# Weight sums of a seven-product up projection: from VectorE to accumulating DMAs, and one product accumulated onto another's negative

## The chip, the cores and the metric

The kernel runs on one core of one Trainium2 chip. The metric is the time of one execution in device microseconds (us). The engines in the profile: PE is TensorE (matmuls; PEld its weight loads), DVE is VectorE, ACT is ScalarE, POOL is GpSimd, SP is SyncE, which issues nearly all DMAs.

## The reference

One inference step of a decoder with two layers, for a prompt of 1024 positions and 8 samples of 8 positions, 1088 columns in all; the model has 1024 rows. Each layer is a mixer (layer 0: convolution and retention, layer 1: a gated recurrence), then a gated feed-forward network (FFN) with a causal depthwise convolution of width 3 between its projections. The change touches only the first product of the FFN, `h @ w_up`, and the RMS norm in front of it:

```python
def _conv_ffn(h, buf, w_up, conv_w, conv_b, w_down):
    z = h @ w_up
    zc, new_buf = _causal_dwconv(z, buf, conv_w, conv_b)
    g, u = jnp.split(zc, 2, axis=-1)
    return (jax.nn.gelu(g) * u) @ w_down, new_buf
...
        x = x + y
        hn = _rmsnorm(x, p['norm_ffn'][l])
        y, fb = _conv_ffn(hn, ffn_buf[l], p['w_ffn_up'][l], p['ffn_conv_w'][l], p['ffn_conv_b'][l], p['w_ffn_down'][l])
```

`w_up` is 1024 x 5632: 22 blocks of 128 columns for g and 22 for u.

## The kernel before, in words

**Exact products.** All data is fp32. A value is split into a high part (a ScalarE copy to fp32r) and a low part (VectorE: the value less its high part), and a product is three matmuls: high x high, high x low, low x high (`mm3`, L227; each matmul is issued at L222). So each weight tile of 128 x 512 costs one ScalarE copy (L119) and one VectorE subtraction (L137, or L167 in the up stage).

**The up stage with seven products.** A pair p takes the blocks p (g) and 22 + p (u) of `w_up`, each 128 x 1024 for the two halves of the 1024 rows: a11, a12 (rows' halves of the first block) and a21, a22 (of the second). The activations are halved in the same way by rows and by columns (544 columns each). This is a 2 x 2 block product, done by Winograd's form of Strassen's scheme with 7 products in place of 8, each on sums of weight blocks and sums of activation blocks. One product is four row blocks of 128, so 12 matmuls of 272 columns, done for each of two ranges of columns (sb 0 and 1): 168 matmuls a pair, and there are 22 pairs in a layer.

**Weight sums.** `Pair.steps` (L161) loads both blocks into `raw` tiles (L124, by SP; three such buffers) and makes seven weight tiles W[0] to W[6] in turn, one a `yield`: a11; a11 - a21; a21 + a22; a21 + a22 - a11; a12; a22; a12 less the fourth. The sums are VectorE adds on 128 x 512 (L172, L175, L180, L185). While pair p is multiplied, pair p + 1's weights are made: three during the first `four`, four during the second (`make_first`, `make`).

**Activation sums.** `norm_halves` (L316) normalises one of three column blocks (208, 208, 128 columns of each half): ScalarE squares and VectorE sums (L331), TensorE transposes the sums (L341), VectorE reduces (L342), ScalarE takes the root (L343), VectorE the reciprocal (L344), TensorE broadcasts it (L351), VectorE scales X (L357), and then four splits and three sums or more per row group follow (`put`, `diff`; L368, L369, L374). The plain blocks go to HB, the sums to HX.

**Products.** `four` (L524) does the products of W[0] to W[3] of one column range, `three` (L546) those of W[4] to W[6], which accumulate onto banks of the first four (p1, p7, p5). MOVE (L484) says which activation block goes with which weight. After the first product ScalarE copies its bank into u2 (L530) and W[4]'s product may then accumulate onto the bank; after the fourth, VectorE adds: u2 += p6 (L540), u3 = u2 + p7 (L541), and the results z are written by L511, L513, L553, L556.

**What sets the order.** The code is written in program order with `side` generators that are advanced by a count of matmuls; a scheduler then orders each engine's instructions by priority and by what is free. Each engine runs its own in order, and so does the queue of DMAs that each issues. The FFN starts while the last block of the projection before it is still being normalised: `proj_tail` (L405) calls `ffn.start()` (both `raw` loads of pair 0), makes the first weights during its third block, and appends the norms of blocks 0, 1 and 2 to `side`. At L588 the rest of pair 0's weights are made, all norms but the last are finished, and the first products run beside block 2's norm. Since `three` of pair 0 stands ahead of the second `four` there (L620 to L624), block 2's norm ends between them.

**Banks.** PSUM has five banks in pool mmp and three in axp, the latter also used by the transposes of the norms.

## Time and profile before

| | us |
|---|---|
| median of 3 runs (lowest, highest) | 2309.07 (2307.93, 2309.26) |
| the profiled execution | 2310.94 |
| its span | 2309.2 |
| up stage, steady part, layer 0 and layer 1 | 527 to 970 and 1592 to 2035 |
| start of the up stage, layer 0 and layer 1 | about 485 to 527 and 1552 to 1592 |

The span is what the trace covers, 1.7 us less than the time measured for the same execution; its mean TensorE clock was 0.989 of full speed. Rows of the trace give a start in us from the span's start, a duration in us, the engine, the line of the kernel, the operation, out<-in by the program's names, the size, and in brackets how long the engine had waited and for what. Durations of neighbouring VectorE and ScalarE instructions overlap by some hundredths or tenths of a us, so the step from one start to the next is the cost of one in a row.

### The profile page before, as it was taken

What the parts mean: (1) busy time and instruction counts of PE and PEld (TensorE: products, weight loads), DVE (VectorE), ACT (ScalarE), POOL (GpSimd) and SP (SyncE); (2) the same over time, 40 slices, a digit from 0 to 9 for tenths busy, and PEclk for the clock granted to TensorE, in tenths of its full rate; (3) what the DMA queues carried; (4) which work ended last, traced back from release to release, by engine and by line L of the source; (5) the groups of instructions that cost most, each with busy time, mean ns of one, the idle gap of its engine ahead of it and who ended that gap; (6) DMA issues with size and microseconds to landing.
All of it is one profiled execution on the core that took longest, in us unless ns stands there. A gap on an engine that the chain in (4) does not pass through costs nothing.

```text
span 2309.2 us, 38057 instructions
## 1 busy us (share of the span) xinstructions
PE 2265.7 (98%) x15428; PEld 2230.5 (97%) x15428; DVE 1650.1 (71%) x2945; ACT 1018.6 (44%) x2082; POOL 37.5 (2%) x65
## 2 busy tenths in 40 slices
PE   9999999989999999999999999999999999999998
PEld 8999999979999999999999999998999999999998
DVE  6899975499888888844337766569888888763425
ACT  6344436445444444622125766435454444442212
POOL 0000000000000000000000121000000000000000
PEclk9999999989999999999999999999999999999999
DMA  5212113222221222454123111422322221264302
GB/s 196 68 40 69 45 55 97 74 67 85 95 85 67 75 85 80 152 169 138 58 74 105 37 38 46 124 73 62 110 68 75 85 84 67 84 210 138 97 19 78
DMA packets 114672, 200.37 MB, mean 87 GB/s; under 512 B 27136, under 2 KB 81280, under 8 KB 114368
## 3 DMA queue, kind: packets, MB, share of 16 engines
q1 hardware_dynamic: 114496, 197.94, 27.2%
q8 instruction: 121, 1.98, 0.4%
q14 instruction: 55, 0.45, 0.1%
HBM read 151.70 MB, written 46.21 MB: 86 GB/s over the span
## 4 chain that ended last, share of the span: by engine, by line
PE 90%; DVE 6%; ACT 2%; DMA 1%; issue 1%; DVEq 0%; SPq 0%; ACTq 0%
PE mm L222 72%; PE ax L222 14%; DVE X L357 1%; DVE acc L331 1%; DVE HB L369 0%; DVE td L374 0%; PE ax L1190 0%; DVE xe L1075 0%; PE ax L882 0%; DVE HX L369 0%; PE ax L873 0%; DMA X<-in_x 0%; PE ax L864 0%; PE ax L844 0%; PE ax L832 0%
## 5 line engine op out<-in xcount | busy, mean ns | idle before, releaser
L222 PE MATMUL mm<-HB,ws 128*128 128x384 f32 (+4 forms) x9504 | 1536.7, 317 | 12.9 <-ACT HB L368 5.6
L222 PEld LDWEIGHTS mm<-HB,ws 128*128 128x128 f32 x9504 | 1464.3, 189 | 27.1 <-ACT HB L368 7.8
L119 ACT ACTIVATE ws<-raw 128x512 fp32r<-128x512 f32 x472 | 289.1, 620 | 337.4 <-PE mm L222 232.0
L167 DVE TENSOR_TENSOR ws<-raw,ws 128x512 fp32r<-128x512 f32 x264 | 180.1, 686 | 71.6 <-ACT ws L119 69.4
L222 PE MATMUL mm<-HX,ws 128*128 128x272 f32 x1584 | 228.0, 293 | 0.3 <-ACT HX L368 0.2
L222 PE MATMUL ax<-HX,ws 128*128 128x272 f32 x1584 | 222.6, 289 | 0.0
L222 PEld LDWEIGHTS mm<-HX,ws 128*128 128x128 f32 x1584 | 212.6, 193 | 1.5 <-ACT HX L368 0.8
L222 PEld LDWEIGHTS ax<-HX,ws 128*128 128x128 f32 x1584 | 208.1, 188 | 0.0
L137 DVE TENSOR_TENSOR ws<-raw,ws 128x512 fp32r<-128x512 f32 x208 | 135.5, 665 | 79.2 <-ACT ws L119 78.5
L263 DVE TENSOR_TENSOR X<-X,mm 128x384 f32<-128x384 f32 (+1 forms) x132 | 69.7, 529 | 150.9 <-PE mm L222 142.5
L750 DVE SCALAR_TENSOR_TENSOR X<-U,par,X 128x1024 f32<-128x1024 f32 x120 | 151.3, 1275 | 0.0
L222 PE MATMUL ax<-HB,ws 128*128 128x272 f32 x1056 | 145.5, 287 | 0.0
L222 PE MATMUL mm<-A,ws 128*128 128x384 f32 (+1 forms) x864 | 142.7, 327 | 0.0
L222 PEld LDWEIGHTS mm<-A,ws 128*128 128x128 f32 x864 | 142.4, 188 | 0.0
L222 PEld LDWEIGHTS ax<-HB,ws 128*128 128x128 f32 x1056 | 136.9, 188 | 0.0
L566 DVE SCALAR_TENSOR_TENSOR X<-X,par 128x1104 f32<-128x1104 f32 x88 | 119.7, 1360 | 0.7 <-ACT X L565 0.5
L565 ACT ACTIVATE X<-X,par 128x1104 f32<-128x1104 f32 x88 | 114.3, 1298 | 5.6 <-DVE X L556 5.6
L567 DVE SCALAR_TENSOR_TENSOR X<-X,par 128x1104 f32<-128x1104 f32 x88 | 116.6, 1360 | 0.0
L553 ACT ACTIVATE X<-mm 128x272 f32<-128x272 f32 x88 | 35.0, 397 | 180.2 <-PE mm L222 180.2
L572 ACT ACTIVATE X<-X 128x1024 f32<-128x1024 f32 x44 | 46.7, 1061 | 45.0 <-DVE X L567 45.0
L500 ACT ACTIVATE X<-fst 128x16 f32<-128x16 f32 x88 | 18.3, 213 | 96.8 <-DVE X L567 96.8
L586 DVE TENSOR_TENSOR A<-yl,A 128x544 fp32r<-128x544 f32 x24 | 17.4, 725 | 60.3 <-ACT A L585 60.3
(236 smaller groups left out, 1929.3 us busy)
## 6 DMA issues: line engine op xcount, KB each, us to landing
raw<-in_w SPq DMA_DIRECT2D x176, 512.0 KB, 3.8
yd<-X SPq DMA_DIRECT2D x44, 544.0 KB, 2.7
yl<-yd SPq DMA_DIRECT2D x88, 272.0 KB, 3.4
spf<-X SPq DMA_DIRECT2D x4, 1664.0 KB, 6.9
xr<-spf SPq DMA_DIRECT2D x32, 208.0 KB, 3.0
raw<-in_w SPq DMA_DIRECT2D x16, 384.0 KB, 4.1
X<-in_xt SPq DMA_DIRECT2D x8, 512.0 KB, 7.1
X<-in_x SPq DMA_DIRECT2D x4, 768.0 KB, 5.3
```

What stands on the lines that cost most here:

```text
L119: nc.scalar.activation(hi, src, AF.Copy)
L137: nc.vector.tensor_tensor(lo, src, hi.bitcast(F32), ALU.subtract)
L167: nc.vector.tensor_tensor(lo, src, hi.bitcast(F32), ALU.subtract)
L222: nc.tensor.matmul(out, lhsT, rhs, start=start, stop=stop, skip_group_check=more)
L263: nc.vector.tensor_tensor(X[:, m, t0:t0 + n], X[:, m, t0:t0 + n], ps[:, :n], ALU.add)
L331: nc.vector.tensor_tensor(acc[:, :N], acc[:, :N], sq[:, :N], ALU.add)
L553: nc.scalar.activation(low(z1, sb), p1[:, :n], AF.Copy)
L565: nc.scalar.activation(y, z[:, 2:NE], AF.Identity, bias=pc(fb, f), scale=pc(fw, 2 * 44 + f))
L566: v.scalar_tensor_tensor(y, z[:, 1:NE - 1], pc(fw, 44 + f), y, ALU.mult, ALU.add)
L567: v.scalar_tensor_tensor(y, z[:, 0:NE - 2], pc(fw, f), y, ALU.mult, ALU.add)
L572: nc.scalar.activation(YG[:, :NP], y[:, :NP], AF.Gelu_apprx_tanh)
L750: nc.vector.scalar_tensor_tensor(cv, U[i][:, j:j + NP], wj, cv, ALU.mult, ALU.add)
```

## The change

Three things, in `Pair`, `norm_halves` and `four`/`three`.

1. The weight sums are made by DMAs that GpSimd issues with `accum_op=ALU.add`: each reads 128 x 512 of a weight block from DRAM and adds it onto half a `raw` tile. There are four a pair, here called A to D. To have sums only, the scheme's signs change: W[0] to W[6] are a11; a21 + a22 (A is issued when the pair is loaded); a11 + a21 (B, after W[0] is split); a11 + a21 + a22 (C, after W[1] is split); a12; a22; the sum of all four (D, after W[3] is split). The four VectorE adds and the tile s3 are gone. Primes (w0', w1') mark the weights of the pair after the one that is multiplied.
2. The activation sums change sign with them (`diff` takes an operation), and W[1] and W[2] change places in MOVE.
3. For pairs from the third on, ScalarE copies the negated bank of W[0]'s product, a, into the bank b (L547 after the change), W[3]'s product accumulates onto it, and ScalarE copies b out as u (L549). For the first two pairs, W[3]'s product has its own bank; ScalarE copies it into u3 (L544) and VectorE forms u = u3 - a (L545). The VectorE add L540 and the copy L530 are gone. W[4]'s product still accumulates onto a.

```diff
+            self.add(1, 0, 1, 1)
             self.gen = self.steps()
 
+        def part(self, j, h):
+            return self.raws[j][:, h * 512:(h + 1) * 512]
+
+        def add(self, j, h, q, g):
+
+            nc.gpsimd.dma_start(self.part(j, h), I["w"][self.i + q][:, g * 512:(g + 1) * 512], accum_op=ALU.add)
+
+        def put(self, j, h):
+            src = self.part(j, h)
+            w, hi, lo = split_w(src)
+            nc.vector.tensor_tensor(lo, src, hi.bitcast(F32), ALU.subtract)
+            self.w.append(w)
+
         def steps(self):
...
-            v.tensor_tensor(s3, a11, a21, ALU.subtract)
-            put(a11)
+            self.put(0, 0)
+            self.add(0, 0, 1, 0)
             yield
-            v.tensor_tensor(a21, a21, a22, ALU.add)
-            put(s3)
+            self.put(1, 0)
+            self.add(1, 0, 0, 0)
             yield
-            put(a21)
+            self.put(0, 0)
             yield
-            v.tensor_tensor(a11, a21, a11, ALU.subtract)
-            put(a11)
+            self.put(1, 0)
+            self.add(1, 0, 0, 1)
             yield
-            put(a12)
+            self.put(0, 1)
             yield
-            v.tensor_tensor(a12, a12, a11, ALU.subtract)
-            put(a22)
+            self.put(1, 1)
             yield
-            put(a12)
+            self.put(1, 0)
...
-            MOVE = (0, 5, 1, 4, 2, 6, 3)
+            MOVE = (0, 1, 5, 4, 2, 6, 3)
...
-                p1 = bank()
-                product(W.w[0], 0, sb, p1, True)
-                nc.scalar.activation(u2[:, :n], p1[:, :n], AF.Copy)
+                a = bank()
+                product(W.w[0], 0, sb, a, True)
                 after(0)
...
-                p6 = bank2() if sb else bank()
-                product(W.w[3], 3, sb, p6, True)
-                v.tensor_tensor(u2[:, :n], u2[:, :n], p6[:, :n], ALU.add)
-                v.tensor_tensor(u3[:, :n], u2[:, :n], p7[:, :n], ALU.add)
-                high(z2, sb, u3, p5)
+                b, u = bank2(), u2s[sb]
+                if p < 2:
+
+                    product(W.w[3], 3, sb, b, True)
+                    nc.scalar.activation(u3[:, :n], b[:, :n], AF.Copy)
+                    v.tensor_tensor(u[:, :n], u3[:, :n], a[:, :n], ALU.subtract)
+                else:
+                    nc.scalar.activation(b[:, :n], a[:, :n], AF.Copy, scale=-1.0)
+                    product(W.w[3], 3, sb, b)
+                    nc.scalar.activation(u[:, :n], b[:, :n], AF.Copy)
+                v.tensor_tensor(u3[:, :n], u[:, :n], f[:, :n], ALU.add)
+                high(z2, sb, u3, e, ALU.subtract)
```

Line numbers shift: L222 becomes L225, L167 (low half) becomes L172, and L167 is now the accumulating DMA; L331 to L357 become L334 to L360, L369 becomes L372, L374 becomes L377, L553 becomes L561. The order in which the start of layer 0 now stands on the two engines that matter there is shown in the prediction. One place more, on ScalarE, layer 0, around the root of block 1's norm; before:

```order
L330 ACTIVATE sq_4542<-X_84 128x416
L119 ACTIVATE ws_4731<-raw_4212 128x512
L119 ACTIVATE ws_4778<-raw_4734 128x512
L343 ACTIVATE r_4557<-r_4557,epst_83 128x4
L368 ACTIVATE HB_85<-X_84 128x2x208 x3
L368 ACTIVATE HX_4184<-td_4606 128x2x208
```

and after:

```order
L333 ACTIVATE sq_4543<-X_84 128x416
L119 ACTIVATE ws_4730<-raw_4214 128x512
L119 ACTIVATE ws_4775<-raw_4733 128x512
L346 ACTIVATE r_4558<-r_4558,epst_83 128x4
L371 ACTIVATE HB_85<-X_84 128x2x208 x3
L119 ACTIVATE ws_4799<-raw_4735 128x512
L371 ACTIVATE HX_4184<-td_4606 128x2x208
L371 ACTIVATE HB_85<-td_4610 128x2x208
L119 ACTIVATE ws_4845<-raw_4733 128x512
```

ws_4731 and ws_4730 are W[6] of pair 0, ws_4778 and ws_4775 W[0] of pair 1, ahead of the root in both; W[1] and W[2] of pair 1 (ws_4799, ws_4845) have moved up among the splits of block 1.

More of the change, by code (lines that the diff above doesn't have):

```diff
@@ L369, in put, with diff @@
                 nc.vector.tensor_tensor(lo, src, hi.bitcast(F32), ALU.subtract)
-            def diff(x, y):
+            def diff(x, y, op=ALU.subtract):
                 t = tmpp.tile([P, 544], F32, tag="tmp", name="td")
                 tv = t[:, :N].rearrange("p (k c) -> p k c", k=2)
-                nc.vector.tensor_tensor(tv, x, y, ALU.subtract)
+                nc.vector.tensor_tensor(tv, x, y, op)
                 return tv
             put(b11, kk, 0)
-            t3 = diff(b22, b12)
+            t3 = diff(b12, b22)
             put(t3, None, 3)
-            t1 = diff(b12, b11)
+            t1 = diff(b11, b12)
             put(t1, kk, 1)
-            t2 = diff(b22, t1)
+            t2 = diff(b22, t1, ALU.add)
             put(t2, None, 2)
@@ L457, in pair @@
         def pair(self, p):
-            return Pair(self.up, [("up%d" % self.l, p), ("up%d" % self.l, NFF + p)])
+            return Pair([("up%d" % self.l, p), ("up%d" % self.l, NFF + p)])
         def run(self, norm_next, final):
@@ L481, in moving, with product @@
                 return HX[:, e, i - 4, k, o:o + n]
-            MOVE = (0, 5, 1, 4, 2, 6, 3)
-            def product(w, i, sb, ps, first):
+            MOVE = (0, 1, 5, 4, 2, 6, 3)
+            def product(w, i, sb, ps, first=False):
                 o, n = SB[sb]
@@ L526, in four @@
                 n = SB[sb][1]
-                u2, z2 = u2s[sb], Zs[2 * (p % 2) + 1]
-                p1 = bank()
-                product(W.w[0], 0, sb, p1, True)
-                nc.scalar.activation(u2[:, :n], p1[:, :n], AF.Copy)
+                z2 = Zs[2 * (p % 2) + 1]
+                a = bank()
+                product(W.w[0], 0, sb, a, True)
                 after(0)
-                p7 = bank2() if sb else bank()
-                product(W.w[1], 1, sb, p7, True)
+                e = bank2() if sb else bank()
@@ L534, in four @@
+                product(W.w[1], 1, sb, e, True)
                 after(1)
-                p5 = bank2() if sb else bank()
-                product(W.w[2], 2, sb, p5, True)
+                f = bank()
+                product(W.w[2], 2, sb, f, True)
                 after(2)
-                p6 = bank2() if sb else bank()
-                product(W.w[3], 3, sb, p6, True)
-                v.tensor_tensor(u2[:, :n], u2[:, :n], p6[:, :n], ALU.add)
-                v.tensor_tensor(u3[:, :n], u2[:, :n], p7[:, :n], ALU.add)
@@ L543, in four @@
+                v.tensor_tensor(u3[:, :n], u[:, :n], f[:, :n], ALU.add)
+                high(z2, sb, u3, e, ALU.subtract)
                 after(3)
-                banks[sb] = p1, p7, p5
+                banks[sb] = a, e, f, u
             def three(p, W, sb, after):
                 n = SB[sb][1]
-                u2 = u2s[sb]
                 z1, z2 = Zs[2 * (p % 2)], Zs[2 * (p % 2) + 1]
-                p1, p7, p5 = banks.pop(sb)
-                product(W.w[4], 4, sb, p1, False)
-                nc.scalar.activation(low(z1, sb), p1[:, :n], AF.Copy)
+                a, e, f, u = banks.pop(sb)
@@ L554, in three @@
+                product(W.w[4], 4, sb, a)
+                nc.scalar.activation(low(z1, sb), a[:, :n], AF.Copy)
                 after(4)
-                product(W.w[5], 5, sb, p7, False)
-                v.tensor_tensor(low(z2, sb), u2[:, :n], p7[:, :n], ALU.add)
+                product(W.w[5], 5, sb, f)
+                v.tensor_tensor(low(z2, sb), u[:, :n], f[:, :n], ALU.add)
                 after(5)
-                product(W.w[6], 6, sb, p5, False)
-                high(z1, sb, u2, p5)
+                product(W.w[6], 6, sb, e)
@@ L560, in three @@
+                high(z1, sb, e, u, ALU.subtract)
                 after(6)
```

20 lines of the change are left out of this document (6 added, 14 removed).

## The prediction

> **What bounds the kernel now.** I read the page first, then busy times by stage, then the chain of waits, then the timelines of the two starts of the up stage. The page:
>
> ```profile
> span 2309.2 us, 38057 instructions
> PE 2265.7 (98%) x15428; PEld 2230.5 (97%) x15428; DVE 1650.1 (71%) x2945; ACT 1018.6 (44%) x2082; POOL 37.5 (2%) x65
> ```
>
> TensorE is the bound as a whole. By stage (start:end, length, then each engine's busy us, the granted clock, the DMA share and GB/s):
>
> ```profile
> 482.00:486.00 4.00, 3.03 (x26) 2.83 (x24) 4.00 (x9) 1.10 (x2) 0.00 (x0) 1.00 1.08 345
> 500.00:527.00 27.00, 23.44 (x144) 22.36 (x145) 24.13 (x62) 15.07 (x41) 0.00 (x0) 0.81 0.00 1
> 527.00:970.00 443.00, 443.00 (x3533) 443.00 (x3532) 375.25 (x624) 216.41 (x455) 0.00 (x0) 1.00 0.27 87
> 1566.00:1592.00 26.00, 21.32 (x145) 19.88 (x145) 25.21 (x64) 15.60 (x42) 0.00 (x0) 0.93 0.01 1
> 1592.00:2035.00 443.00, 443.00 (x3533) 443.00 (x3532) 375.25 (x624) 216.36 (x455) 0.00 (x0) 1.00 0.27 87
> ```
>
> In the steady part of both up stages TensorE is busy all 443.00 us at full clock, with VectorE at 375.25. Only at the two starts (500 to 527, 1566 to 1592) does TensorE wait, and there VectorE is nearly full. The steady chain, one pair of column blocks:
>
> ```profile
> 738.44 7.54 PE mm L222 x60
> 745.99 4.51 PE ax L222 x36
> 750.49 6.04 PE mm L222 x48
> 756.53 2.99 PE ax L222 x24
> ```
>
> That is 21.08 us for 168 matmuls, 0.1255 us each, and 0.1257, 0.1253, 0.1258, 0.1246 in the four pieces. The pace doesn't follow what VectorE does meanwhile. So what is taken off VectorE in the steady part (four adds of 0.68 us and two of 0.43 a pair, rows below, of its 375.25/443.00 x 21.08 = 17.9 us) is worth nothing there, and two more ScalarE copies of 0.40 us a pair (L553's row below; it is busy 216.41) cost nothing unless TensorE waits for them.
>
> **The two starts, where the change decides.** On TensorE in layer 0, before: between block 1's norm and block 2's (L341, L351) stand the products of W[0] to W[4]. W[2], W[3], W[4] are ws_4665, ws_4669, ws_4698; mm_4738 is the bank of the first product:
>
> ```order
> L222 MATMUL mm_4805<-HB_85,ws_4665 128x272 x5
> L222 MATMUL mm_4850<-HX_4184,ws_4669 128x272 x6
> L222 MATMUL mm_4738<-HB_85,ws_4698 128x272 x12
> L341 MATMUL ax_4789<-ident_82,acc_4746 128x128 x2
> L222 MATMUL mm_4781<-HX_4184,ws_4702 128x272 x12
> L351 MATMUL ax_4818<-ident_82,r_4788 128x128 x2
> L222 MATMUL mm_4805<-HB_85,ws_4731 128x272 x12
> L222 MATMUL mm_4935<-HB_85,ws_4575 128x272
> ```
>
> After, block 2's L344 and L354 follow on W[2] directly, and the product of W[4] (again mm_4738<-ws_4698) stands here:
>
> ```order
> L225 MATMUL ax_4983<-HX_4184,ws_4668 128x272
> L225 MATMUL ax_5103<-HX_4184,ws_4947 128x272 x2
> L225 MATMUL ax_4983<-HX_4184,ws_4668 128x272 x4
> L225 MATMUL mm_4738<-HB_85,ws_4698 128x272 x12
> L225 MATMUL mm_4803<-HX_4184,ws_4701 128x272 x12
> L225 MATMUL mm_4779<-HB_85,ws_4730 128x272 x12
> ```
>
> It has moved from ahead of block 2's norm to behind the second column half (mm_4934 to ax_4983) and the first of pair 1 (ax_5103). The reason is on VectorE. For the first two pairs the change forms u = u3 - a (L545), which reads bank a = mm_4738; W[4]'s product accumulates into that bank, so it must wait for L545. On VectorE after, at the end of block 2's norm:
>
> ```order
> L377 TENSOR_TENSOR td_4875<-X_84,td_4869 128x256
> L372 TENSOR_TENSOR HX_4184<-td_4869,HX_4184 128x2x128
> L545 TENSOR_TENSOR X_84<-X_84,mm_4738 128x272
> L172 TENSOR_TENSOR ws_4947<-raw_4735,ws_4947 128x512
> L372 TENSOR_TENSOR HX_4184<-td_4875,HX_4184 128x2x128
> L550 TENSOR_TENSOR X_84<-X_84,mm_4803 128x272
> ```
>
> L545 stands behind the whole of block 2's norm, where before ScalarE's copy freed the bank at once. So the products of W[4] to W[6] and pair 1's fill (mm_5054, mm_5073, mm_5090) are gone from the wait: until block 2's last but one split is done TensorE can do 36 (W[0] to W[2]) + 12 (W[3]) + 45 (second half, and two of ax_5103) = 93 matmuls, and no more. Matmuls of L222 done by then, before:
>
> ```profile
> 491.80:524.75 32.95, 27.48 (x147) 0.75 0.11 36
> 1559.00:1591.96 32.96, 27.55 (x164) 0.84 0.12 38
> ```
>
> **When block 2 is ready after.** VectorE and ScalarE rows of layer 0, then layer 1:
>
> ```profile
> 483.21 0.68 DVE L167 TENSOR_TENSOR ws<-raw,ws 128x512 fp32r<-128x512 f32 x1
> 505.00 0.42 DVE L331 TENSOR_TENSOR acc<-acc,sq 128x256 f32<-128x256 f32 x1
> 506.17 0.68 DVE L172 TENSOR_TENSOR s<-raw 128x512 f32<-128x512 f32 x1
> 506.77 0.42 DVE L331 TENSOR_TENSOR acc<-acc,sq 128x256 f32<-128x256 f32 x1
> 508.65 0.42 DVE L331 TENSOR_TENSOR acc<-acc,sq 128x256 f32<-128x256 f32 x1
> 509.82 0.69 DVE L167 TENSOR_TENSOR ws<-raw,ws 128x512 fp32r<-128x512 f32 x1 [0.76 <-ACT ws L119]
> 510.77 0.43 DVE L540 TENSOR_TENSOR X<-X,mm 128x272 f32<-128x272 f32 x1
> 511.12 0.42 DVE L331 TENSOR_TENSOR acc<-acc,sq 128x256 f32<-128x256 f32 x1
> 515.44 1.65 DVE L357 SCALAR_TENSOR_TENSOR X<-X,par,ax 128x256 f32<-128x256 f32 x4
> 525.28 0.42 DVE L369 TENSOR_TENSOR HX<-td,HX 128x256 fp32r<-128x256 f32 x1
> ```
> ```profile
> 487.03 1.15 ACT L119 ACTIVATE ws<-raw 128x512 fp32r<-128x512 f32 x2 [3.15 <-DVE raw L185]
> ```
> ```profile
> 1550.43 0.68 DVE L167 TENSOR_TENSOR ws<-raw,ws 128x512 fp32r<-128x512 f32 x1
> 1572.21 0.41 DVE L331 TENSOR_TENSOR acc<-acc,sq 128x256 f32<-128x256 f32 x1
> 1577.49 0.41 DVE L331 TENSOR_TENSOR acc<-acc,sq 128x256 f32<-128x256 f32 x1
> 1580.47 1.65 DVE L357 SCALAR_TENSOR_TENSOR X<-X,par,ax 128x256 f32<-128x256 f32 x4
> 1590.31 0.42 DVE L369 TENSOR_TENSOR HX<-td,HX 128x256 fp32r<-128x256 f32 x1
> ```
> ```profile
> 1554.24 1.15 ACT L119 ACTIVATE ws<-raw 128x512 fp32r<-128x512 f32 x2 [3.15 <-DVE raw L185]
> ```
>
> (a) The sixth weight sum, w6, needs the last add. Before, VectorE makes it (L185) and ScalarE splits it at 487.03. After, it is the fourth accumulating DMA (D), which may start when w3's low half is done, 483.21 + 0.68 = 483.89. Its split stands ahead of block 1's square root on ScalarE, and its low half ahead of the reciprocal on VectorE (ws_4730, with ws_4775 pair 1's w0'):
>
> ```order
> L172 TENSOR_TENSOR ws_4701<-raw_4214,ws_4701 128x512
> L416 TENSOR_TENSOR X_84<-X_84,mm_4704 128x2x128
> L345 TENSOR_REDUCE r_4558<-ax_4559 128x4
> L172 TENSOR_TENSOR ws_4730<-raw_4214,ws_4730 128x512
> L347 RECIPROCAL r_4558<-r_4558 128x4
> L172 TENSOR_TENSOR ws_4775<-raw_4733,ws_4775 128x512
> ```
>
> In before ws_4731 stood behind the reciprocal. So block 1's reciprocal, all its splits, and block 2 behind them wait for D. No accumulating DMA is in the trace of before. The nearest rows, on the page and for the weight tiles from 425 to 560 us:
>
> ```profile
> raw<-in_w SPq DMA_DIRECT2D x176, 512.0 KB, 3.8
> xr<-spf SPq DMA_DIRECT2D x32, 208.0 KB, 3.0
> ```
> ```profile
> DMA to landing us min/median/max: 3.4/4.0/7.0
> ```
> ```profile
> 480.05 0.54 SPq L321 DMA_DIRECT2D spf<-X  x1
> ```
>
> D moves 256 KB, but reads its target too; bounds 3.0 (xr) and 7.0. In 482 to 486 the DMA engines are full (share 1.08: the spill of L321, issued at 480.05), so I take 5.5 us, halfway from 4.0 to 7.0: D lands at 489.4, 2.4 us after 487.03. In layer 1, 1551.11 + 5.5 = 1556.6 against 1554.24, again 2.4. A sentence of its own: the Trainium skill, "DMA: Bandwidth & Descriptors", section "Anatomy of one DMA — SWDGE (gpsimd) path", fits a DMA from GpSimd at 2.0 us + bytes/436e3, which would be 2.6 us here and would put nothing between w6 and its place; no run here shows it yet, and by it the loss below would be 9.6 + 1.6 + 1 = 12 us.
>
> (b) Pair 1's w1' and w2' splits, which stood among block 2's sums of squares, now stand among block 1's splits on ScalarE: 1.15 for two by the row of 487.03, some of it in ScalarE's gaps: 0.8. So δ = 2.4 + 0.8 = 3.2 us, bounds 0.5 and 5.5 (D at 3.4 and at 7.0).
>
> (c) Block 2's sums of squares ran from 505.00 to 511.12 + 0.42 = 511.54, 6.54 us. Gone from between: L172 (506.77 - 506.17 = 0.60) and L175 the same, the wait before 509.82 (509.82 - 508.65 - 0.34 = 0.83) and L540 (511.12 - 510.77 = 0.35). Left: 4.16. Layer 1 has no such wait: 1577.90 - 1572.21 = 5.69, less 1.53 = 4.16. (d) From there to L357: before 3.90 and 2.57; the late one had TensorE in the way, so 2.3, a little under the smaller. (e) L357 to the end of the last but one split: 525.70 - 515.44 = 10.26, in layer 1 too.
>
> TensorE gets on at 505.00 + 4.16 + 2.3 + 10.26 + δ = 521.72 + δ = 524.9 with 93 matmuls done, where before had 147 at 524.75: 54 x 0.1257 + 0.15 = 6.9 us behind. Layer 1: 1572.21 + 16.72 + 3.2 = 1592.1, where before had 164 at 1591.96: 71 x 0.1257 + 0.17 = 9.1 us. Together 16.0, or 9.6 + 2δ. Nothing later gives it back, since TensorE has no idle time in 527 to 970. What the clock adds: it sinks while TensorE waits, and the twelve of W[5] took in layer 0 and in layer 1
>
> ```profile
> 511.99 3.05 PE L222 MATMUL mm<-HX,ws 128*128 128x272 f32 x12
> ```
> ```profile
> 1578.30 1.77 PE L222 MATMUL mm<-HX,ws 128*128 128x272 f32 x12
> ```
>
> so 1.3 us for one slow dozen; I add 1 in all (bounds 0 and 3). The sum is +17 us (bounds 10 and 23): 2310.94 for the profiled execution, which is 1.9 over the median 2309.07, becomes 2328, and the median 2326.
>
> **The steady part after.** Two new waits. W[3]'s product of a pair waits for ScalarE's L547 (b = -a), and L547 stands behind w2' hi, which waits for the second add (B); B waits for w0' to be split:
>
> ```profile
> 756.57 0.40 ACT L553 ACTIVATE X<-mm 128x272 f32<-128x272 f32 x1 [3.87 <-PE mm L222]
> 756.86 0.62 ACT L119 ACTIVATE ws<-raw 128x512 fp32r<-128x512 f32 x1
> ```
> ```profile
> 757.52 0.69 DVE L167 TENSOR_TENSOR ws<-raw,ws 128x512 fp32r<-128x512 f32 x1 [1.76 <-ACT ws L119]
> ```
> ```profile
> 763.89 1.67 PE L222 MATMUL mm<-HX,ws 128*128 128x272 f32 x12
> ```
>
> B may start at 757.52 + 0.69 = 758.21; w2' hi and L547 take 0.92 (0.62 + 0.40, overlapping by some 0.1), and W[3]'s product starts at 763.89 with 0.09 of handing over: B has 4.67 us. In the free DMA of this part (share 0.27) I take 4.1 (a 512 KB load's 3.8 and some for the second read), and nothing is lost; each us over 4.67 costs one us in each of about 19 periods a layer, 38 in all. The other adds have slack or make only ScalarE wait.
>
> **The rivals.** First, the steady stall: B takes over 4.67 us. For it: all four adds pass POOL's one queue, and 7.0 is in the rows; against it, medians of 3.0 and 3.8. At 5.2 it is 38 x 0.53 = 20 us more, 2346; at 5.5, 2357. The Trainium skill, "SBUF — State Buffer", in its warning on VectorE blocking DMA, says that GpSimd can't write descriptors while VectorE runs a two-port mode; that would be this rival, and no run here shows it.
>
> Second, faster: the pace of 0.1257 us might hold something that VectorE's PSUM and SBUF traffic adds, and fewer VectorE operations would quicken it. If 3 ns of each of 2 x 22 x 168 = 7392 matmuls went, 22 us less, 2304 with the start loss; it decides at 2.3 ns. Against it: 0.1253 to 0.1258 in pieces where VectorE does quite different work.
>
> Third, no change: the start loss at its low bound of 10, and the second rival's gain at 1.4 ns (7392 x 1.4 = 10 us): 2309. It asks for two unlikely things at once.
>
> **How the numbers follow.** Forecast 0.62, stall 0.25, no change 0.06, faster 0.07. Range: 2316 (the forecast's low bound, rounded down from 2319 for a shorter (d)) to 2360, the stall at (2360 - 2326)/38 = 0.9 over 4.67; beyond it lies a quarter of the stall. 0.13 + 0.06 are left out. Within 0.2% (4.6 us, what a measurement of this kernel can tell from none) is the third rival; slower 0.62 + 0.25 = 0.87.
>
> **What would show it.** Right: D landing 5 to 6 us after 483.9; L545 after block 2's splits with twelve mm_4738<-ws_4698 waiting for it; TensorE idle several us before 525 and 1592; the pair period still 21.08. Wrong: a period over 21.1 (the stall, with W[3]'s product released by L547) or under 21.0 (the faster rival), or W[4]'s product running before block 2's L344.

## The result, and the profile after

| | before | after |
|---|---|---|
| median, us (lowest, highest) | 2309.16 (2307.93, 2309.86) | 2390.47 (2389.37, 2398.53) |
| the profiled execution, us | 2310.94 | 2389.37 |
| its span, us | 2309.2 | 2387.6 |
| ratio of the medians (95% interval) | | 1.036 (1.0337 to 1.0383) |

The change makes the kernel 81 us slower. The prediction said slower, by 17 us, with a range that ended at 2360; the result lies 30 us outside it.

The page of the kernel after, for the span, the engines, the chain of waits by engine, and the weight DMAs (KB each and the median us from issue to landing):

```profile
span 2387.6 us, 38404 instructions
PE 2287.7 (96%) x15428; PEld 2242.5 (94%) x15428; DVE 1522.6 (64%) x2689; ACT 1038.8 (44%) x2162; POOL 189.8 (8%) x241
PE 59%; DMA 17%; DVE 12%; issue 6%; ACT 5%; POOL 0%; POOLq 0%; SPq 0%; DVEq 0%; ACTq 0%
...
raw<-in_w SPq DMA_DIRECT2D x176, 512.0 KB, 4.5
raw<-in_w POOLq DMA_DIRECT2D x176, 256.0 KB, 5.0
```

VectorE lost 127 us of work and it bought nothing: 17% of the chain that ended last is now DMA (1% before). An accumulating DMA of 256 KB takes 5.0 us in the median, longer than a load of 512 KB, and the loads have become slower too (4.5 us; 3.8 before).

Where the time went is read from four marks of each layer: block 1's transposes, where the up stage starts, and the fourth and the last of the DMAs that write back the results of a pair (`yd<-X`), 18 pairs apart. In the kernel before, on TensorE and on SP's queue:

```profile
486.48 0.63 PE L341 MATMUL ax<-ident,acc 128*128 128x128 f32 x4 [1.45 <-DVE acc L331]
...
1553.60 0.66 PE L341 MATMUL ax<-ident,acc 128*128 128x128 f32 x4 [0.40 <-DVE acc L331]
```
```profile
600.44 0.33 SPq L577 DMA_DIRECT2D yd<-X  x1
...
983.56 0.32 SPq L577 DMA_DIRECT2D yd<-X  x1
...
1665.48 0.33 SPq L577 DMA_DIRECT2D yd<-X  x1
...
2049.54 0.32 SPq L577 DMA_DIRECT2D yd<-X  x1
```

and in the kernel after:

```profile
482.61 0.63 PE L344 MATMUL ax<-ident,acc 128*128 128x128 f32 x4 [1.45 <-DVE acc L334]
...
1589.85 0.66 PE L344 MATMUL ax<-ident,acc 128*128 128x128 f32 x4 [0.41 <-DVE acc L334]
```
```profile
615.77 0.33 SPq L585 DMA_DIRECT2D yd<-X  x1
...
1018.99 0.32 SPq L585 DMA_DIRECT2D yd<-X  x1
...
1721.45 0.33 SPq L585 DMA_DIRECT2D yd<-X  x1
...
2127.34 0.32 SPq L585 DMA_DIRECT2D yd<-X  x1
```

| | layer 0 before, after | layer 1 before, after | lost |
|---|---|---|---|
| start: transposes to fourth store | 113.96, 133.16 | 111.88, 131.60 | 19.2 + 19.7 = 38.9 |
| steady: fourth to last store, 18 pairs | 383.12, 403.22 | 384.06, 405.89 | 20.1 + 21.8 = 41.9 |

The two make 80.8. The span is only 78.4 us longer, because this execution of after reached the first mark 3.9 us earlier and lost 1.5 elsewhere. The forecast had 17 for the starts and nothing for the steady part.

**The steady part.** The same stretch of 340 us before, then after (busy us of PE, PEld, DVE, ACT, POOL with counts, then the clock, DMA share, GB/s):

```profile
620.00:960.00 340.00, 340.00 (x2713) 340.00 (x2712) 282.73 (x467) 162.49 (x342) 0.00 (x0) 1.00 0.25 80
```
```profile
620.00:960.00 340.00, 325.70 (x2554) 322.41 (x2553) 218.78 (x347) 157.54 (x351) 53.08 (x61) 0.99 0.54 121
```

TensorE is no longer full. 2554 matmuls at 340.00/2713 = 0.1253 us would be 320.1 us: 14.3 of the 19.9 us lost are idle, and the other 5.6 lie in the matmuls next to the waits. The last one before a wait and the first one after it show longer, for no other runs beside them, and behind the wait that ended at 810.73 fifteen matmuls took 0.227 us each, with a granted clock of 0.51 in 812.00 to 815.30. The waits of TensorE and of ScalarE in that stretch (us in total, times, longest):

```profile
PE ax L225 <- ACT ax L547: 14.2, 13, 2.2
```
```profile
ACT ws L119 <- DMA raw<-in_w: 96.9, 29, 5.5
```

Nearly all of TensorE's waiting (14.2 of 14.3 us) is for L547, the copy that puts -a into W[3]'s bank; and ScalarE, busy under half of the time, stands 96.9 of 340 us before weights that an add has not yet finished. One period, from ScalarE, SP, VectorE, POOL and TensorE, in order of time (the L119 at 755.14 splits w6, at 756.43 w0', at 764.06 w2'; L172 at 757.11 is the low half of w0'; L167 at 758.20 is B):

```profile
755.14 0.63 ACT L119 ACTIVATE ws<-raw 128x512 fp32r<-128x512 f32 x1 [5.41 <-DMA raw<-in_w]
...
756.43 0.63 ACT L119 ACTIVATE ws<-raw 128x512 fp32r<-128x512 f32 x1
756.52 0.33 SPq L124 DMA_DIRECT2D raw<-in_w  x1
...
757.11 0.68 DVE L172 TENSOR_TENSOR ws<-raw,ws 128x512 fp32r<-128x512 f32 x1
...
758.20 0.86 POOL L167 DMA_DIRECT2D raw<-in_w  x1 [2.83 <-DVE X L564]
...
761.19 1.66 PE L225 MATMUL mm<-HX,ws 128*128 128x272 f32 x12
...
764.06 0.63 ACT L119 ACTIVATE ws<-raw 128x512 fp32r<-128x512 f32 x1 [2.43 <-DMA raw<-in_w]
764.60 0.38 ACT L547 ACTIVATE ax<-mm 128x272 f32<-128x272 f32 x1
...
765.03 1.77 PE L225 MATMUL ax<-HX,ws 128*128 128x272 f32 x12 [2.18 <-ACT ax L547]
```

and the same B, and the B of the next period, as pieces of the chain of waits:

```profile
758.20 5.78 DMA raw<-in_w
...
781.15 5.05 DMA raw<-in_w
```

W[3]'s product waits for L547, L547 stands on ScalarE behind the split of w2', and that split waits for B. B's 4.67 us are overrun in three ways: POOL takes the add up 0.41 us after the low half ends (757.79 to 758.20; the bracket names the VectorE instruction that ended last, but the 0.41 us from the low half is the same for the adds C and D), B itself runs 5.78 us beside the load that SP issued at 756.52, and w0' is 0.6 us late because ScalarE has just waited for D (755.14). 0.41 + 5.78 - 4.67 + 0.6 = 2.1, against 2.18 waited. In the next period B takes 5.05 and w0' is on time: 0.41 + 5.05 - 4.67 = 0.8, against 0.88. Eleven of the 13 waits are of this kind. In the other two (741.50 and 810.73, 2.1 us each) the late split ahead of L547 is that of w1', which A feeds; A took 5.6 and 5.7 us there.

**The starts.** Layer 0 after; this execution is 486.48 - 482.61 = 3.87 us earlier than that of before. The add D and the split that waits for it on POOL and ScalarE, then VectorE from the end of block 2's sums on, then TensorE:

```profile
480.62 0.89 POOL L167 DMA_DIRECT2D raw<-in_w  x1 [10.49 <-ACT sq L333]
...
485.95 1.15 ACT L119 ACTIVATE ws<-raw 128x512 fp32r<-128x512 f32 x2 [5.95 <-DMA raw<-in_w]
...
508.15 2.02 DVE L334 TENSOR_TENSOR acc<-acc,sq 128x256 f32<-128x256 f32 x4
...
512.81 1.65 DVE L360 SCALAR_TENSOR_TENSOR X<-X,par,ax 128x256 f32<-128x256 f32 x4 [0.85 <-PE ax L354]
...
523.12 0.44 DVE L545 TENSOR_TENSOR X<-X,mm 128x272 f32<-128x272 f32 x1
...
523.87 1.68 PE L225 MATMUL mm<-HB,ws 128*128 128x272 f32 x12
```

and the products of L225 from the first on HB to that one (PE and PEld, then the clock, DMA share, GB/s):

```profile
490.64:523.87 33.23, 20.42 (x97) 17.64 (x98) 0.69 0.15 25
```

W[4]'s product (523.87) waits for L545, and L545 for block 2's splits, as forecast; 97 matmuls were done by then, where the forecast had 93 and the kernel before 147. What the forecast didn't have comes after that, within the first three pairs; on TensorE:

```profile
553.20 1.78 PE L225 MATMUL mm<-HX,ws 128*128 128x272 f32 x12 [1.58 <-DVE X L550]
...
565.36 2.55 PE L225 MATMUL ax<-HX,ws 128*128 128x272 f32 x12 [4.36 <-ACT ax L547]
```

The second is the steady stall at its longest, by way of A: A was issued at 553.74 and took 7.5 us, and the split of w1' waited for it (561.34, after 6.59 us) ahead of L547. The first is the same kind of wait with VectorE as the hand between.

### The profile page after: what moved, and what is told of

Read it like the earlier page. It is cut to its first block, busy times and chain, and to the rows that moved or that the text cites. A ratio compares the mean times of both kernels' runs of the same rounds, so it can differ in the third digit from the quotient of the medians.

```text
span 2387.6 us, 38404 instructions
## 1 busy us (share of the span) xinstructions
PE 2287.7 (96%) x15428; PEld 2242.5 (94%) x15428; DVE 1522.6 (64%) x2689; ACT 1038.8 (44%) x2162; POOL 189.8 (8%) x241
## 4 chain that ended last, share of the span: by engine, by line
PE 59%; DMA 17%; DVE 12%; issue 6%; ACT 5%; POOL 0%; POOLq 0%; SPq 0%; DVEq 0%; ACTq 0%
PE mm L225 51%; DMA raw<-in_w 16%; PE ax L225 3%; DVE ws L172 3%; DVE X L574 2%; DVE X L575 2%; ACT X L580 1%; ACT ws L119 1%; DVE acc L334 1%; DVE X L360 1%; ACT X L573 1%; DVE HB L372 0%; DVE HX L372 0%; DVE td L377 0%; POOL raw L167 0%
## 5 line engine op out<-in xcount | busy, mean ns | idle before, releaser
L225 PE MATMUL mm<-HB,ws 128*128 128x384 f32 (+4 forms) x9504 | 1536.7, 318 | 20.1 <-ACT HB L371 12.6
L225 PEld LDWEIGHTS mm<-HB,ws 128*128 128x128 f32 x9504 | 1469.1, 190 | 35.8 <-ACT HB L371 15.0
L119 ACT ACTIVATE ws<-raw 128x512 fp32r<-128x512 f32 (+1 forms) x516 | 316.8, 620 | 597.0 <-PE mm L225 283.8
L172 DVE TENSOR_TENSOR ws<-raw,ws 128x512 fp32r<-128x512 f32 x308 | 212.2, 690 | 285.4 <-ACT ws L119 285.0
L225 PE MATMUL mm<-HX,ws 128*128 128x272 f32 x2112 | 300.4, 290 | 2.6 <-DVE X L550 2.6
L225 PEld LDWEIGHTS mm<-HX,ws 128*128 128x128 f32 x2112 | 279.4, 190 | 3.8 <-DVE X L550 3.0
L167 POOL DMA_DIRECT2D raw<-in_w x176 | 153.3, 871 | 1163.7 <-DVE X L584 357.3
L225 PE MATMUL ax<-HX,ws 128*128 128x272 f32 x1056 | 157.3, 300 | 37.1 <-ACT ax L547 37.0
L225 PEld LDWEIGHTS ax<-HX,ws 128*128 128x128 f32 x1056 | 142.9, 195 | 45.0 <-ACT ax L547 44.8
L137 DVE TENSOR_TENSOR ws<-raw,ws 128x512 fp32r<-128x512 f32 x208 | 135.7, 668 | 76.2 <-ACT ws L119 75.6
L225 PE MATMUL ax<-HB,ws 128*128 128x272 f32 x1056 | 146.3, 287 | 0.0
L225 PE MATMUL mm<-A,ws 128*128 128x384 f32 (+1 forms) x864 | 142.7, 327 | 0.0
L225 PEld LDWEIGHTS mm<-A,ws 128*128 128x128 f32 x864 | 142.4, 188 | 0.0
L225 PEld LDWEIGHTS ax<-HB,ws 128*128 128x128 f32 x1056 | 137.4, 189 | 0.4
L549 ACT ACTIVATE X<-ax 128x272 f32<-128x272 f32 x80 | 31.9, 399 | 96.5 <-PE ax L225 96.5
L583 DVE TENSOR_TENSOR X<-X 128x1024 f32<-128x1024 f32 x44 | 53.9, 1225 | 11.7 <-ACT X L580 11.7
```

Source lines behind the costliest of these rows:

```text
L119: nc.scalar.activation(hi, src, AF.Copy)
L137: nc.vector.tensor_tensor(lo, src, hi.bitcast(F32), ALU.subtract)
L167: nc.gpsimd.dma_start(self.part(j, h), I["w"][self.i + q][:, g * 512:(g + 1) * 512], accum_op=ALU.add)
L172: nc.vector.tensor_tensor(lo, src, hi.bitcast(F32), ALU.subtract)
L225: nc.tensor.matmul(out, lhsT, rhs, start=start, stop=stop, skip_group_check=more)
L583: v.tensor_tensor(YG[:, :NP], YG[:, :NP], y[:, :NP], ALU.mult)
```

## The experiments

Each kernel is an edit of the kernel after, if nothing else is said. "Ratio" is to the kernel before on the same chip, with a 95% interval; that kernel's median was 2308.98 to 2311.03 in the five sets.

**1. e1_later_w2: one split later.** W[2] to W[6] of the next pair are each split one product later, so that W[2]'s split, which stood in front of L547, goes into the second `four` and W[6]'s behind the product of W[4].

```diff
                 def make_first(i):
-                    if i < 3:
+                    if i < 2:
                         make(i)
+
+                def make_sixth(i):
+                    if i == 4:
+                        make(i)
...
-                    three(p, W, 0, nothing)
+                    three(p, W, 0, make_sixth)
...
+                    make(4)
                     three(p, W, 1, last)
```

> All as in the changed kernel, but the next pair's W[2] to W[6] are each made one product later, so that on ScalarE the negated copy L547 of the first column range no longer stands behind W[2]'s split, which waits for DMA B. Theory 1 (ScalarE's queue: L547 waits behind the split that waits for B, and TensorE's W[3] product waits for L547): the 48 us that the 18 steady periods of each layer lost (402.2 and 404.7 us in place of 379.4) go, and most of the waits of 4.4 and 2.9 us in pair 2, so 2333 to 2345 us. Rival (the adds' traffic itself slows TensorE or the weights come too late for it): the adds are all still there, so 2380 to 2395 us, with TensorE waiting for weights or running over 0.126 us a matmul.

Measured: 2359.96 (2349.16 to 2366.99), ratio 1.0211 (1.018 to 1.0243). Neither theory's number: 30 of the 81 us come back. (The 48 us of the expectation are counted from 18 times 21.08 us; against the 383 to 384 us that 18 pairs take in the kernel before, the steady loss is 41.9.) On ScalarE and TensorE in the third pair:

```profile
559.15 0.63 ACT L119 ACTIVATE ws<-raw 128x512 fp32r<-128x512 f32 x1 [5.90 <-DMA raw<-in_w]
...
562.66 2.64 PE L225 MATMUL ax<-HX,ws 128*128 128x272 f32 x12 [4.02 <-ACT ax L547]
```

L547 itself ran at 562.23. B's split has gone from ahead of it, and another split that an add feeds (w1', fed by A) is now the one that ScalarE is held by. The wait was handed on, less often and less evenly: TensorE waits for L547 5 times in 620 to 960, 5.8 us in all, against 13 times and 14.2 us.

**2. e2_own_bank: no L547 at all.** W[3]'s product keeps its own bank in every pair.

```diff
-                if p < 2:
+                if True:
 
                     product(W.w[3], 3, sb, b, True)
```

> All pairs take the way of the first two: W[3]'s product has a bank of its own, ScalarE copies it out and VectorE subtracts W[0]'s bank; there is no L547. The accumulating DMAs stay as they are. Theory 1: W[3]'s product no longer waits for ScalarE, the steady loss goes, 2335 to 2348 us. Rival (the adds' traffic or late weights): 2380 to 2395 us.

Measured: 2386.4 (2383.01 to 2391.2), ratio 1.0331 (1.0314 to 1.0349). My theory, that only L547 turns the late add into a stall, fell here. ScalarE, VectorE and TensorE in one period (the split is w6, which D feeds; L516 empties a bank of the products):

```profile
778.00 0.63 ACT L119 ACTIVATE ws<-raw 128x512 fp32r<-128x512 f32 x1 [6.04 <-DMA raw<-in_w]
778.66 0.69 DVE L172 TENSOR_TENSOR ws<-raw,ws 128x512 fp32r<-128x512 f32 x1 [5.46 <-ACT ws L119]
...
779.55 0.21 DVE L516 TENSOR_TENSOR X<-X,ax 128x64 f32<-128x64 f32 x1
...
779.82 1.75 PE L225 MATMUL ax<-HB,ws 128*128 128x272 f32 x12 [0.76 <-DVE X L516]
```

The late split holds its low half on VectorE for 5.46 us, the low half holds L516 behind it, and TensorE waits for the bank. So an instruction that empties a bank on VectorE did here what L547 did on ScalarE.

**3. e3_vector_sums: the adds back on VectorE.** The new signs, the new order of products and the accumulation onto W[0]'s negative stay; only the accumulating DMAs go.

```diff
-            self.put(0, 0)
-            self.add(0, 0, 1, 0)
...
+            v.tensor_tensor(s3, a11, a21, ALU.add)
+            self.put(a11)
             yield
-            self.put(1, 0)
-            self.add(1, 0, 0, 0)
+            v.tensor_tensor(a21, a21, a22, ALU.add)
+            self.put(a21)
...
-            self.put(1, 0)
-            self.add(1, 0, 0, 1)
+            v.tensor_tensor(a11, a21, a11, ALU.add)
+            self.put(a11)
...
```

> The products and signs of the changed kernel, but the weight sums are made by VectorE as in the kernel before (four adds of 128x512 a pair); no accumulating DMA. Theory 1: L547 still stands behind W[2]'s split on ScalarE, but that split waits for no DMA, so there is no steady loss; the two starts lose what L545 takes from TensorE (9.6 us by the prediction's sum with no delay of the norm, up to 15): 2318 to 2328 us. Rival (the accumulation onto the negated copy is itself too slow for TensorE): 2345 us or more with waits for L547 in each period.

Measured: 2326.21 (2325.69 to 2326.55), ratio 1.007 (1.0053 to 1.0087), inside what was expected. The steady stretch is full again, with the new bank path in it:

```profile
620.00:960.00 340.00, 340.00 (x2713) 340.00 (x2712) 273.33 (x432) 172.76 (x372) 0.00 (x0) 1.00 0.24 78
```

So 64 of the 81 us belong to the accumulating DMAs, among them all of the steady loss. Between the same marks the two starts lose 6.2 and 8.4 us here: the products' and the bank's part of the change.

**4. e4_bank_free: the bank freed at once.** For the first two pairs ScalarE copies W[0]'s bank away, and VectorE subtracts the copy, so that W[4]'s product needn't wait for L545.

```diff
                 product(W.w[0], 0, sb, a, True)
+                if p < 2:
+                    nc.scalar.activation(u2s[sb][:, :n], a[:, :n], AF.Copy)
                 after(0)
...
-                    v.tensor_tensor(u[:, :n], u3[:, :n], a[:, :n], ALU.subtract)
+                    v.tensor_tensor(u[:, :n], u3[:, :n], u[:, :n], ALU.subtract)
```

> As the changed kernel, but in the first two pairs ScalarE copies W[0]'s bank out at once and VectorE subtracts the copy, so W[4]'s product need not wait for L545. If L545 is what holds W[4]'s product at the two starts, TensorE can do about 21 to 24 matmuls more per layer while block 2 is normalised: 5 to 6 us less, 2384 to 2386 us. Rival (the starts lose through the late norm alone): no change, 2389 to 2392 us.

Measured: 2388.4 (2384.79 to 2392.29), ratio 1.0339 (1.0321 to 1.0357). The runs spread over 7.5 us and the two theories are 3 apart: inconclusive. In the profiled execution the starts lost 19.7 and 23.3 us, no less than in the kernel after.

**5. e5_last_late: another order of the splits.** In program order W[6] is split after the first product of its own pair, and the next pair's splits come one place later.

```diff
                 def make_first(i):
-                    if i < 3:
+                    if i == 0:
+                        W.make()
+                    elif i < 3:
                         make(i)
```

> All as in the changed kernel, but all splits of the next pair stand one product later and W[6]'s split is made after the first product of its own pair, so that each split stands at least 4 us behind the add that feeds it (D: some 10 us). Theory 1, widened after the first four runs (a split that waits for any of the adds holds up ScalarE and VectorE, in order, and with them the bank that TensorE needs next): nearly all of the steady loss goes, also what was left with W[2] to W[6] later, 2330 to 2348 us. Rival (three load buffers make the weights late, whatever the order): 2355 us or more.

Measured: 2363.75 (2358.05 to 2376.81), ratio 1.0235 (1.0202 to 1.0268): missed. On ScalarE only w2' has come behind L547: w1' still stands ahead of it, and w6 still waits over 5 us for D. Most periods are whole, and a few stall hard. ScalarE and TensorE (the split is w1', fed by A):

```profile
799.14 0.63 ACT L119 ACTIVATE ws<-raw 128x512 fp32r<-128x512 f32 x1 [4.75 <-issue]
...
802.65 2.99 PE L225 MATMUL ax<-HX,ws 128*128 128x272 f32 x12 [2.20 <-ACT ax L547]
```

Here A was issued at 793.30, late because the load that it adds onto had taken 6.25 us, and took 5.8 us itself; it landed 0.1 us before the split began. That made me suspect late loads, with three `raw` buffers for two pairs; runs 9 and 12 test it.

**6. e6_vector_bank_free: runs 3 and 4 together,** to see the bank's price without the DMAs.

> The kernel with VectorE's sums (2326.2, all of its loss at the two starts), and in the first two pairs ScalarE copies W[0]'s bank out at once. If L545 holds W[4]'s product at the starts, TensorE has 21 to 24 matmuls more per layer during block 2's norm: 2 x 2.6 to 3.0 = 5 to 6 us less, 2320 to 2321. Rival (the starts lose by the place of the W[3] product and the norm alone): 2325 to 2327 us.

Measured: 2319.27 (2318.37 to 2321.68), ratio 1.0039 (1.0026 to 1.0052), 6.9 us under run 3. The wait for L545 costs 7 us. The starts still lose 4.3 and 5.2.

**7. e7_sums_only: the adds alone.** The DMAs stay; W[3]'s product has its own bank and ScalarE frees W[0]'s bank at once in every pair, so what TensorE waits for is nearly as before the change.

```diff
+                if True:
+                    nc.scalar.activation(u2s[sb][:, :n], a[:, :n], AF.Copy)
                 after(0)
...
-                if p < 2:
+                if True:
...
-                    nc.scalar.activation(u3[:, :n], b[:, :n], AF.Copy)
-                    v.tensor_tensor(u[:, :n], u3[:, :n], a[:, :n], ALU.subtract)
+                    v.tensor_tensor(u[:, :n], b[:, :n], u[:, :n], ALU.subtract)
```

> The first part of the change alone: the sums by accumulating DMAs with the new signs, while for all pairs ScalarE copies W[0]'s bank out at once, W[3]'s product has its own bank and VectorE subtracts, as in the kernel before. Theory 1: the splits that wait for D and B still hold up the evictions of VectorE and ScalarE, so nearly the steady loss of the kernel with its own banks stays, 2375 to 2390 us. Rival (the accumulation onto the negated copy is the cause and own banks only moved the wait): under 2350 us.

Measured: 2380.1 (2368.82 to 2383.99), ratio 1.029 (1.0262 to 1.0318), as expected: 70 of the 81 us with the old bank path. Run 3 takes the DMAs out and has 64 by difference; this one leaves them alone in. The two agree.

**8. e8_late_free: runs 4 and 5 together.**

> Later splits as in the run e5_last_late and the early copy of W[0]'s bank in the first two pairs. Theory 1: what e5_last_late gives, less 4 to 6 us at the starts. Rival: as e5_last_late.

Measured: 2354.28 (2352.41 to 2356.53), ratio 1.0188 (1.0171 to 1.0205), 9.5 us under run 5, more than the 4 to 6 expected, but run 5's own runs spread over 19 us.

**9. e9_four_loads: a fourth `raw` buffer,** for which the pool of split weights gives up one of ten slots.

```diff
-    wpool = ctx.enter_context(tc.tile_pool(name="wpool", bufs=10))
-    rawp = ctx.enter_context(tc.tile_pool(name="rawp", bufs=3))
+    wpool = ctx.enter_context(tc.tile_pool(name="wpool", bufs=9))
+    rawp = ctx.enter_context(tc.tile_pool(name="rawp", bufs=4))
```

> The changed kernel with four load buffers in place of three and nine slots for split weights in place of ten (the same memory). Each load, and with it add A, can start about a period earlier, and each split stands one slot later on ScalarE. Theory 1 (splits that wait for adds A, B, D hold up ScalarE and VectorE): waits of ScalarE for raw<-in_w fall from 97 us in 620 to 960 to under 40, and the time to 2340 to 2365 us. Rival (the adds' traffic as such): 2380 us or more. The mixers run with the same two numbers changed and may move by some us themselves.

Measured: 2337.35 (2335.11 to 2337.72), ratio 1.0118 (1.0102 to 1.0134), a little better than expected. The steady loss is gone. But two things were changed, so run 12 changes one.

**10. e10_plain_dma: the same DMAs without the addition.** They read, and overwrite; the sums of weights are left out.

```diff
-            nc.gpsimd.dma_start(self.part(j, h), I["w"][self.i + q][:, g * 512:(g + 1) * 512], accum_op=ALU.add)
+            nc.gpsimd.dma_start(self.part(j, h), I["w"][self.i + q][:, g * 512:(g + 1) * 512])
```

> The 176 DMAs of GpSimd without the addition: each writes its 256 KB block over the target, with the same waits and order (the sums are left out). If the accumulation is what makes them long (an add alone took 3.7 to 4.0 us from issue to landing, 5.0 in the median), the median falls to 3 us or less and the time to under 2350 us; if issue, queue and collisions with the loads are, the median stays at 4.3 or more and the time over 2370.

Measured: 2379.54 (2378.41 to 2380.67), ratio 1.0303 (1.0278 to 1.0328). From its page:

```profile
raw<-in_w POOLq DMA_DIRECT2D x176, 256.0 KB, 3.7
```

A plain DMA takes 3.7 us in the median where the accumulating one takes 5.0, and 11 of the 81 us go with that. Neither theory's pair of numbers came: the median lies between the two, the time with the second. The other 70 us remain with no addition in any DMA, so the addition is not the main thing. The trace adds what the medians hide. Between 620 and 960 TensorE waits 14.2 us for L547, as much as in the kernel after, but no longer through B: B took 3.8 and 2.8 us (issued at 758.18 and 780.25), well under its 4.67. A is late in its place, behind a load of 5.5 us, and the split of w1' waits for it (POOL's A, the split, W[3]'s product):

```profile
756.02 0.54 POOL L167 DMA_DIRECT2D raw<-in_w  x1 [5.97 <-DVE ws L172]
...
760.30 0.63 ACT L119 ACTIVATE ws<-raw 128x512 fp32r<-128x512 f32 x1 [3.25 <-issue]
...
764.34 1.76 PE L225 MATMUL ax<-HX,ws 128*128 128x272 f32 x12 [0.72 <-ACT ax L547]
```

On the size: the Trainium skill, "DMA: Bandwidth & Descriptors", section "Anatomy of one DMA — SWDGE (gpsimd) path", fits a DMA from GpSimd at 2.0 us + bytes/436e3, which gives an estimate of 2.6 us for these. The medians here differ, and the measurement decides: 3.7 plain, 5.0 accumulating; the shortest plain one between 620 and 960 took 2.7.

**11. e11_four_late_free: runs 4, 5 and 9 together.**

> Four load buffers and nine weight slots, W[6]'s split after the first product of its own pair and the others one product later, and the early copy of W[0]'s bank in the first two pairs. Theory 1: every add has several us more than it takes, so the steady part runs at 21.08 us a pair but for rare waits, and only the two starts lose: 2322 to 2340 us. Rival (traffic as such): as e9_four_loads.

Measured: 2339.91 (2338.81 to 2339.96), ratio 1.013 (1.0111 to 1.0148). The steady part is whole as in run 9, and the reorderings bring nothing more at the starts; the upper edge of what was expected.

**12. e12_nine_slots: only the slot.** Three `raw` buffers as in the kernel after, nine slots for split weights.

```diff
-    wpool = ctx.enter_context(tc.tile_pool(name="wpool", bufs=10))
+    wpool = ctx.enter_context(tc.tile_pool(name="wpool", bufs=9))
```

> The changed kernel with nine slots for split weights, three load buffers as it has: of the two edits of the run with four loads only the one that puts the splits a slot later on ScalarE. If it is the late load (raw waits for a buffer, add A waits for the load, the split and the eviction behind it wait for A) that keeps the steady part slow, this regains only a part, 2350 to 2375 us, and the period stays over 21.6 us. If the place of the splits alone did it, 2335 to 2342 us and a period of 21.1 to 21.3.

Measured: 2337.75 (2336.93 to 2338.99), ratio 1.0114 (1.0096 to 1.0133). The theory of late loads fell: one slot less does it alone, with the three load buffers as they were. The steady stretch, and what ScalarE's splits wait for in it:

```profile
620.00:960.00 340.00, 340.00 (x2713) 340.00 (x2712) 237.72 (x373) 172.56 (x372) 54.94 (x63) 1.00 0.55 127
```
```profile
ACT ws L119 <- PE mm L225: 80.9, 49, 3.5
```

Every accumulating DMA is still there (63 issued, DMA share 0.55), and TensorE does 2713 matmuls in 340 us as before the change. With a slot less, a split can't start before TensorE has let go of an older weight, so each comes one place later in ScalarE's order, and by then its add has landed: no split in this stretch waits for a DMA. On ScalarE (w1', L547, L549, then w2'):

```profile
769.23 0.62 ACT L119 ACTIVATE ws<-raw 128x512 fp32r<-128x512 f32 x1
...
770.95 0.38 ACT L547 ACTIVATE ax<-mm 128x272 f32<-128x272 f32 x1
...
775.00 0.40 ACT L549 ACTIVATE X<-ax 128x272 f32<-128x272 f32 x1 [0.78 <-PE ax L225]
...
776.51 0.64 ACT L119 ACTIVATE ws<-raw 128x512 fp32r<-128x512 f32 x1
```

w2' now stands behind L547 and L549. The adds are also shorter here than in the kernel after: D took 4.1 and 4.3 us (758.68, 779.75) where it took 6.4 and 6.6 (748.75, 771.46), and it is now issued 1.4 us behind the store and not 0.2. No run separates this from the place of the splits. But with the longer times of the two periods shown above (D 6.6, B 5.8) D would land at 765.3 and B (issued at 769.25) at 775.0, still ahead of their splits at 765.98 and 776.51. The starts gain only in part: 13.0 and 14.5 us lost, against 19.2 and 19.7.

**13. e13_start_by_vector: nine slots, the bank freed at once, and VectorE's adds for the first two pairs** of a layer; DMAs from the third on.

```diff
+            self.dma = keys[0][1] >= 2
...
-            self.add(1, 0, 1, 1)
-            self.gen = self.steps()
+            if self.dma:
+                self.add(1, 0, 1, 1)
+            self.gen = self.steps() if self.dma else self.vector_steps()
```

> Nine slots for split weights, the early copy of W[0]'s bank in the first two pairs, and VectorE's sums for pairs 0 and 1 of each layer; from pair 2 on the accumulating DMAs as in the changed kernel. If what is left with nine slots (27 us, all at the two starts) is the adds of the first pairs plus L545, about what VectorE's sums with the early copy gave: 2316 to 2324 us. If the nine slots or the adds of later pairs cost it, 2328 us or more.

Measured: 2321.86 (2321.52 to 2322.24), ratio 1.0055 (1.004 to 1.007), as expected. Of run 12's 27 us some 14 are the first pairs' adds and the wait for L545. The 13 us left are about the 9.2 that run 6, with no DMA adds at all, stands over the kernel before, and the price of the slot (next).

**14. e14_before_nine: the kernel before, with nine slots.**

> The kernel before with nine slots for split weights, nothing else. If a slot less has a price of its own (at the starts or in the mixers), it shows here: up to 10 us over the kernel before. If not, 2308 to 2312 us.

Measured: 2311.88 (2310.05 to 2313.55), ratio 1.0013 (1.0003 to 1.0022): a slot costs 3 us (1 to 5 by the interval).

No version here beats the kernel before. TensorE's pace bounds it, and none of the edits gives TensorE less to do.

## Why the prediction was right or wrong

**What bounds the kernel, and what VectorE's relief is worth: right.** In run 12 VectorE is busy 237.72 of 340 us where it was 282.73, and the number of matmuls is the same 2713. The pace does not follow VectorE. The rivals "faster" and "no change" fall with that.

**The starts: the mechanism right, the sum too small.** The terms, forecast and measured in layer 0 (times of after plus 3.87):

| term | forecast | measured | from |
|---|---|---|---|
| D | 5.5 | 5.3 | 480.62 to 485.95 |
| δ, block 2's sums begin later | 3.2 | 4.3 | 505.44 + 3.87 - 505.00 |
| (c) block 2's sums | 4.16 | 4.7 | 505.44 to 508.15 + 2.02 |
| (d) to the scaling of X | 2.3 | 2.6 | to 512.81 |
| (e) to the last but one split | 10.26 | 10.4 | to 523.21 |
| L545 and the start of W[4]'s product | 0 | 0.7 | 523.21 to 523.87 |

TensorE gets on at 523.87 + 3.87 = 527.74 with 97 matmuls done, against 524.75 with 147 before: 50 x 0.1257 + 2.99 = 9.3 us behind, where 6.9 was forecast. In layer 1 the same product starts at 1631.46, or at 1595.21 once the 36.25 us that the layer begins late are taken off, with 97 done, against 1591.96 with 164: 8.4 + 3.25 = 11.7 us, where 9.1 was forecast. So this step gave 16.0 and measured 21.0. The other 18 of the starts' 38.9 us were not in the sum at all: between TensorE's getting on and the fourth store, 662 and 663 matmuls took 91.9 and 90.0 us in place of 83.2 and 83.3 (at 0.1257 each), 15 us in the two layers. Of these, 10.7 are waits of TensorE, nearly all in the second and third pair, where the stall had its worst moments (565.36, 4.36 us). The stores also come some 8 matmuls later in the order of work than before, 2 us; half a us is unassigned.

**The steady part: the step that failed.** It was "In the free DMA of this part (share 0.27) I take 4.1 ... and nothing is lost". The need was right: B has 4.67 us. The duration was wrong twice. An add with no other load, store or add in flight does take 3.9 to 4.2 us (those issued at 739.23 and 808.46), so 4.1 was a fair price for the one case that the loads of before could show. But the part isn't free after the change: the adds themselves double the DMA share to 0.54, B meets the 512 KB load that SP issues 1.7 us ahead of it (756.52 in the period above), and in the two periods above it takes 5.05 and 5.78; and POOL's hand-over of 0.41 was not in the sum. The first rival, "steady stall", had this mechanism and this price: 38 periods times the excess. At the 1.16 us a period that was lost (41.9/36), it is what happened. Its chance of 0.25 was argued down by medians of 3.0 and 3.8 from a profile that had no adds in it; the share of DMA that the change itself adds, four DMAs of 256 KB that read and write beside two loads of 512 KB, was not worked out.

**"The other adds have slack or make only ScalarE wait": wrong, and it matters more than B's size.** A wait of ScalarE is not free when a copy that frees or fills a bank stands behind it; run 2 shows D doing through VectorE's L516 what B does through L547, and runs 1, 5 and 10 show A in B's place, as do two of the 13 waits of the kernel after itself. Run 10 says how much it matters: there B lands in time, and the steady part loses 19.5 and 19.8 us all the same, against 20.1 and 21.8. That is why undoing one of them brings a part at most (4 us in run 2, 30 in run 1), and why moving all splits one place later wins back the whole steady loss. So the cause of the steady loss, as shown: splits that wait for a DMA, placed in two in-order queues ahead of the work that TensorE needs next. It isn't the traffic as such (run 12 moves the same and loses nothing, though its adds are better spaced), not the addition in the DMA (run 10), and not the number of load buffers (run 12 against run 9).

**The rival of descriptors.** The Trainium skill, "SBUF — State Buffer", in its warning on VectorE blocking DMA, was cited for a GpSimd that can't write descriptors while VectorE runs a two-port mode. No run here isolates it; in run 12 the same VectorE operations run beside the same adds without a stall, so it isn't needed to account for the loss.

What stays open: how the last 9.5 us of the two starts (run 6) divide between the order of products and the norm; how much of run 12's gain is the place of the splits and how much the better spacing of the transfers; and why the granted clock fell after some waits and not after others. A dozen matmuls after a wait of 2.20 us took 2.99 us in run 5, where the granted clock was 0.53 in 802.60 to 805.50, and 1.77 us after a wait of 2.18 in the kernel after (765.03 above), where it was 1.00 in 760 to 768.

## What to carry to other kernels

Before handing an engine's work to a DMA, write down for each engine's queue what stands behind the first instruction that will wait for that DMA, and give the DMA's slack to the nearest instruction there that frees or fills a PSUM bank, not to the DMA's own consumer. Price the DMA with its hand-over and beside the transfers that it will meet, counting the traffic that the change itself adds: the durations of the profile before were too short here (a load took 3.8 us before and 4.5 after). If it is late, move the waiting instructions later as a group (a pool with one slot less did it here; the program order alone, in run 5, did not), and see in the trace that they moved: taking away one of several passes the wait on to the next.
